# A hybrid diffusion step on one core: neighbourhood-attention values computed token-major

## The chip, the cores and the metric

The kernel runs on one core of one Trainium2 chip. The metric is the device time of one execution in microseconds (us). TensorE is called PE here, ScalarE ACT, VectorE DVE, GpSimd POOL, and SyncE, whose queue issues the transfers, SP.

## What is computed

Two trunk layers act on 384 tokens of 1024 features: 128 context tokens and 256 latent tokens. Each layer has a gated feed-forward, a mixer of three parallel branches, and a second feed-forward, each followed by a layer norm. The change concerns branch B of the mixer, attention over a 2-D neighbourhood with 8 heads of 64. Its queries, keys and values come from one input projection, and the values are also an output for the context tokens:

```python
z = h @ w_in
qb, kb, vb = jnp.split(zb, 3, axis=-1)          # zb: the 1536 columns of z for branch B
s = einsum(q, k) * SCALE + bias                 # latent: local window and cached context keys
p = softmax(s); o = einsum(p, v)                # context: full attention over the context
new_na_v = vb of the context tokens
```

## The kernel before

Activations lie feature-major: tile c holds features 128c to 128c+127 on the partitions and the 384 tokens along them. A projection of 128 output features is 8 chunks of 128 input features. Every product is made from two parts of each factor, high and low in the format float32r, as three matmuls: high by high, high by low, low by high. So a projected tile is 24 matmuls with a 128 x 128 weight block stationary and 384 tokens moving (`mm3_steps`, L391; `proj`, L1150). It is issued in four steps of two chunks, and each step reports a cost of 0.96 us to the plan.

Weights are one stream of 128 x 128 blocks in the order of their use (`Stream`, L341). A unit of eight blocks is fetched by one DMA (`raw`), copied by ACT into its high part (`hi`) and subtracted by DVE into its low part (`lo`). Two units of `hi` and `lo` are held, so ACT splits a new unit once PE has made the last product with an old one.

PSUM has eight banks, given out under three tags (L331 to L338): `mm`, three banks, for the dense products; `at`, three, for scores and outputs of the attention; `rw`, two, for transposes and others.

In the mixer, `attention` (L1089) takes eight pairs of heads, 0 to 3 of branch A and 4 to 7 of branch B. A pair (`heads_pair`, L1021) is a generator of eight parts: context scores, latent scores of head 0, transposes, context output, latent scores of head 1, transposes twice, and the output. Between the parts the plan puts steps of dense products. `XP` (L60) lists the dense tiles, first those ahead of the pairs and then those of iterations 0 to 8: "n" is the next projection that a coming pair needs (from `branch_a` and `branch_b`), "c" a projection of branch C with its convolution (`conv_gen`, L1254), "g" a gate, "p" a tile of branch A's output projection. Every letter counts as one tile of 3.84 us ("p" as a half); the sum is spread over eight steps by the weights `WY` (L61), and what is left at the end of an iteration is issued at once. A dense step is issued behind the attention's last instruction on PE so far. Pair m+1 is started in the last of the eight steps of iteration m; if its projections are not yet made, dense steps are issued until they are. The tile scheduler below this sets the final order on each engine.

For each pair of branch B, `branch_b` (L1205) makes three projections: keys (K), values (V) and queries (Q), numbered 0 to 3. The values come out feature-major in PSUM; ACT copies them to `vxb` (L1233), a DMA writes the context part out (L1234), and `token_major` (L990) transposes them with three 128 x 128 transposes on PE into a bank of `rw`, from which ACT copies `vt`, token by feature, which the pair's outputs read. K, V and Q of one pair are three letters "n". The convolution tiles come in the order of `C_FIRST` (L69): tw, al, k0, r0, v0, k1, r1, v1; the norms of a key tile (`kss`, a square root on ACT, L1286) are made within the tile that follows it.

Of the kernel before, what the change touches and what calls it, by code (L numbers as in the profile page):

```python
# [15 lines left out]
P = 128  # L16
# [43 lines left out]
XP = ('gggggg','nc','nggc','nc','nnnc','nnnpppppppp','nnn','nnnc','cc','c')  # L60
# [131 lines left out]
# sets of four groups of 256 modulations; the first two are what the first chunks of features need, then the others  # L192
# [3 lines left out]
def _layout(inp):  # L196
    """Rearranges the inputs (permutations and concatenations only)."""
# [36 lines left out]
    # [l][d][h = (p, e)][v][k] -> [l][(e, k)][p][d][v]  # L234
# [8 lines left out]
def _weights(inp, order):  # L243
    """The large weights as 128 x 128 blocks in the order of their use."""
    f = {k: np.asarray(inp[k]) for k in {o[0] for o in order}}
    arows = np.concatenate([_a_q_cols(m) for m in range(4)])
    n = len(order)
    assert n == WS_UNITS * UNIT
    ws = np.empty((WS_UNITS, P, UNIT, P), next(iter(f.values())).dtype)
    for i, (name, l, k, c) in enumerate(order):  # L250
        rows = arows[P * k : P * k + P] if name == "proj_a" else np.arange(P * k, P * k + P)
        cols = _a_q_cols(c[1]) if isinstance(c, tuple) else slice(c, c + P)
        ws[i // UNIT, :, i % UNIT] = f[name][l, rows][:, cols]
    return ws.reshape(WS_SHAPE)
# [7 lines left out]
    "o_vb": (DEPTH, 4, P, P),  # L262
# [4 lines left out]
def _unlayout(r):  # L267
# [7 lines left out]
    st = r["o_st"].reshape(DEPTH, 2, HD, 4, 2, HD)  # l, e, k, p, d, v  # L275
    st = np.ascontiguousarray(st.transpose(0, 4, 3, 1, 5, 2).reshape(DEPTH, 2, 8, HD, HD))[None]
    return (yp, ys, heads(r["o_ka"], 2), heads(r["o_va"], 2), heads(r["o_kb"], 8), heads(r["o_vb"], 8), st)


class Engine:  # L280
    """An engine that knows its last instruction."""
# [14 lines left out]
def trunk(tc, I, O, order, taps=None, stop=None):  # L296
# [5 lines left out]
    def then(*engines):  # L302
        """Behind the last instruction so far of these engines."""
# [37 lines left out]
    class Stream:  # L341
# [5 lines left out]
        def take(self, name, l, col, n, k0=0):  # L347
            order.extend((name, l, k, col) for k in range(k0, k0 + n))
            while len(self.left) < n:
# [5 lines left out]
            got, self.left = self.left[:n], self.left[n:]  # L355
            return got

        def ahead(self):
            """Out of the steady state: the unit after the next is split as soon as the last is used up."""
            if len(self.left) <= UNIT and self.unit < WS_UNITS:  # L360
                self.fetch(self.offset)
# [4 lines left out]
        def fetch(self, offset=0):  # L366
# [8 lines left out]
            for j in range(0, UNIT * P, n):  # L375
                V.tensor_tensor(out=lo[:, j : j + n], in0=raw[:, j : j + n], in1=hi[:, j : j + n].bitcast(F32), op=ALU.subtract)
            for i in range(UNIT):
                self.left.append((hi[:, i * P : (i + 1) * P], lo[:, i * P : (i + 1) * P]))
# [3 lines left out]
    def mm3(out, chunks, xs, after=()):  # L382
        """out += sum of W_k^T x_k, with both factors as sums of two float32r parts."""
# [7 lines left out]
    def mm3_steps(out, chunks, xs, step=2):  # L391
        """mm3 in steps of a few chunks, with what each costs."""
# [10 lines left out]
    def split(dst_h, dst_l, src, lo_eng):  # L403
        """src (SBUF or PSUM, float32) = dst_h + dst_l."""
# [30 lines left out]
    def ada_beside(pool, n):  # L435
        """The next n steps with the products on the vector engine: where that has time, and the tensor engine has not."""
# [38 lines left out]
    def ada_flush():  # L475
        """To columns: out[feature, (block, group, stream)]."""
# [20 lines left out]
    ax = [act.tile([P, NTOK], F32, name=f"ax{c}") for c in range(KD)]  # L497
    # (four more columns: see Norm)
# [8 lines left out]
    class Norm:  # L507
        """Layer norm over the features of y = alpha x + gate * out, chunk by chunk as out comes.
        The next phase's input is h = rs g1 (y - mu) + b1, g1 and b1 per feature and stream, rs and mu per token. Its
        first products W^T h run on z = g1 y, before rs and mu are known: rs W^T z - rs mu W^T g1 + W^T b1, with g1 and  # L510
        b1 as four more columns of z."""
# [34 lines left out]
        def add(self, c, po):  # L546
# [4 lines left out]
            if c == 0:  # L551
                # the table of Sqrt is there when it is needed
# [27 lines left out]
        def pilot(self):  # L580
            # about the mean of the first four chunks
# [14 lines left out]
        def products(self, chunks, xs, c):  # L596
            """The products of chunk c of out."""
# [14 lines left out]
        def finish(self, head=iter(())):  # L612
            """head: products of the next phase, in steps, from those on z to the last before h is needed."""
# [47 lines left out]
        def h(self, pool, c):  # L661
            """The next phase's input, in two parts."""
# [11 lines left out]
        def x(self):  # L674
            """alpha times the norm's output."""
# [5 lines left out]
    class Head:  # L681
        """The first products of a phase, on z: two groups of them, each chunk by chunk."""
# [25 lines left out]
        def begin(self, pool, norm, job, at):  # L708
            """The start of the phase: h follows the second group's products chunk by chunk; the first group's results."""
# [37 lines left out]
        def scaled(self, key, out, scale=1.0):  # L747
            """out = rs W^T z - rs mu W^T g1; returns scale W^T b1, a column per stream."""
# [21 lines left out]
    def gated(i, l, name, pool, xs, head, after):  # L770
        """128 features of silu(a) g, in two parts."""
# [70 lines left out]
    axd = es.enter_context(tc.tile_pool(name="axd", bufs=1, space=bass.MemoryType.DRAM))  # L842

    def mixer(l, nxt, next_head, head):
        spill = axd.tile([P, KD, NTOK], F32, name=f"axd{l}")
        gcd = axd.tile([P, KD, NTOK], F32, name=f"gcd{l}")
        with ExitStack() as st:
# [9 lines left out]
            with tc.tile_pool(name=f"rw{l}", bufs=1) as pool:  # L857
# [3 lines left out]
                def add(cost, until=None):  # L861
                    """Queues dense work behind the scans' last instruction."""
# [31 lines left out]
    def gate(l, i, m, th, head=None):  # L894
        """tanh(z / 2): the sigmoid is (1 + tanh(z / 2)) / 2."""
# [12 lines left out]
    def project(l, name, m, th, os):  # L908
        """2 merged += 2 gate * (o @ proj); the gate of branch A is in place."""
# [11 lines left out]
    def front_fill(l, keep, pool, w, oa, need, head):  # L921
        """The dense products beside the attention: what its next pair needs, then others."""
# [12 lines left out]

        for plan in XP:
            yield sum(todo[x][0] if x in todo else 1 for x in plan), some(plan)
# [6 lines left out]
    def mixer_fill(l, keep, pool, w, ob, gcd):  # L944
        """Projections without a place in a chain: they keep the tensor engine busy beside the scans."""
# [12 lines left out]
    def softmax(pool, views, nk, sinks):  # L958
        """views: score tiles [P, nk] in PSUM; sinks: [P, n or 1] or None."""
# [22 lines left out]
    def transposed(pe, nk, pts):  # L982
        """pts: P^T destinations [P, nk // P, P]."""
# [6 lines left out]
    def token_major(pool, src, tag):  # L990
        """[128 features, 384 tokens] -> [token, block, feature]."""
# [10 lines left out]
    def key_stack(pool, src, e, bufs):  # L1002
        """Keys of one head, src[64 e :, :384], as [hi; hi] and [lo; lo] over the 128 partitions."""
# [9 lines left out]
    def query_stack(pool, src, e):  # L1013
        """Latent queries of one head, src[64 e :, :256], as [hi; lo] (in either order)."""
# [6 lines left out]
    def heads_pair(pool, q_ctx, q_lat, k_ctx, kst, vt, v_cache, bias, sinks, keep, name, done, backward=False):  # L1021
        """Two heads (on partitions 0..63 and 64..127) of both streams -> o^T split in two parts."""
        # context queries: full attention over the context
# [9 lines left out]
        # latent queries: latent keys, then the cached context keys  # L1033
# [44 lines left out]
    def rope(pool, src, dst):  # L1078
        """Rotates the latent columns of src [128, 384] into dst [128, 256]."""
# [9 lines left out]
    def attention(l, pool, keep, w, oa, ob, head, spill):  # L1089
        """Branches A and B, pair of heads by pair of heads, among steps of the dense products."""  # L1090
# [37 lines left out]
        for m in range(9):  # L1128
# [3 lines left out]
            # two pairs at a time: the first part of one before the end of the other  # L1132
# [31 lines left out]
    def branch_a(l, pool, ready, soon, head):  # L1164
        """Windowed grouped-query attention; pair m has the query heads m and m + 4."""
# [38 lines left out]

    def branch_b(l, pool, ready, soon):  # L1205
        """Neighbourhood attention; latent queries in reverse order: the bias is then a forward walk through na_rpb."""
        cvb = pool.tile([P, 4, P], F32, name="cvb")
        nc.sync.dma_start(out=cvb, in_=I["cvb"][l].rearrange("p (a b) -> p a b", b=P))
        for m in range(4):
# [21 lines left out]
            pz = yield from proj(l, B_V0 + P * m, "pvb")  # L1231
            vx = pool.tile([P, NTOK], F32, tag="vx", bufs=1, name="vxb")
            S.activation(out=vx, in_=pz[:, :NTOK], func=AF.Copy)  # L1233
            nc.sync.dma_start(out=O["o_vb"][l, m], in_=vx[:, :NCTX])  # L1234
            vt = []
            soon.append([LATE, lambda vt=vt, vx=vx: vt.append(token_major(pool, vx, "vt"))])
            yield 0.96
            yield 0.0
# [8 lines left out]
            ready[4 + m] = (qx[:, :NCTX], qx[:, NCTX:], kc, kst, vt[0], cvb[:, m], bias, None)  # L1247
# [4 lines left out]
    C_INDEX = {n: i for i, n in enumerate(["tw", "al", "gl"] + [f"{x}{i}" for x in "krv" for i in range(4)])}  # L1252

    def conv_gen(l, keep, pool, w, names):  # L1254
        """Projections of the scans' inputs with the short convolution over time."""
        wsh = vcol(l, "w_shift")
        late = []
        for nm in names:
# [17 lines left out]
            elif nm[0] == "k":  # L1276
                # 1 / max(|k k_k|, 1e-12) per token and head
# [25 lines left out]
    def head_sums(out, sq):  # L1303
        """out[token, (block, head)] = sums of sq [128 features of two heads, 384] over each head."""
# [3 lines left out]
    def head_spread(pool, rn):  # L1308
        """[token, (block, head)] -> the same for each feature of the head, [128 features, 384], in PSUM."""
# [15 lines left out]
    def beside(k, m, n):  # L1325
        """Dense work beside a product: the tensor engine slows down where it has too little."""
# [464 lines left out]
```

## Time and profile before

| | |
|---|---|
| median of 3 runs | 2436.55 us (2436.5 to 2436.74) |
| span of the profiled execution | 2439.6 us |
| PE busy | 2297.4 us, 94% |
| DVE, ACT, POOL busy | 1696.6, 1056.4, 550.0 us |
| PE's share of the chain that ended last | 71% |

The page gives no time of the profiled execution besides its span. Matmuls are pipelined: a matmul's duration is longer than the distance between the starts of two, so work on PE is counted by starts. An idle time in brackets in the order of time is that of the engine before the instruction, with what ended it.

### The profile page before, as it was taken

How to read it: one execution, taken by the hardware profiler on the slowest of the kernel's cores; microseconds unless marked ns; L12 is line 12 of the kernel's file. 1: busy time of each engine (PE TensorE's matmuls, PEld its weight loads, DVE VectorE, ACT ScalarE, POOL GpSimd, SP SyncE). 2: the span in 40 equal slices, each digit the busy share in tenths (PEclk: the TensorE clock that was granted, in tenths of full speed). 3: DMA queues.
4: the chain of work that ended last, by engine and by line, in shares of the span. 5: the costliest groups of instructions: out<-in, count | busy, mean ns of one | idle time of the engine just before them, and what ended most of it. 6: DMA issues, size and time to landing. Idle time of an engine off the chain costs nothing.

```text
span 2439.6 us, 42863 instructions
## 1 busy us (share of the span) xinstructions
PE 2297.4 (94%) x17066; PEld 2106.5 (86%) x17066; DVE 1696.6 (70%) x2865; ACT 1056.4 (43%) x1942; POOL 550.0 (23%) x522
## 2 busy tenths in 40 slices
PE   7999999998899998999999999899989999999998
PEld 5999988897777788999889999889877777889997
DVE  3797886777767568786978954776787674665534
ACT  3333245655545445333243332555555454443332
POOL 2111422101122044211432113310022220542113
PEclk9999999999999999999999999999999999999999
DMA  8575644242111262665546743523321113534332
GB/s 314 193 240 198 191 122 130 84 111 78 40 57 47 72 209 95 191 217 180 180 147 205 244 130 122 154 81 91 112 70 39 51 50 90 204 102 140 130 121 87
DMA packets 125079, 324.54 MB, mean 133 GB/s; under 512 B 31568, under 2 KB 50256, under 8 KB 124880
## 3 DMA queue, kind: packets, MB, share of 16 engines
q1 hardware_dynamic: 124880, 321.81, 41.1%
q8 instruction: 134, 2.20, 0.4%
q14 instruction: 65, 0.53, 0.1%
HBM read 312.06 MB, written 9.70 MB: 132 GB/s over the span
## 4 chain that ended last, share of the span: by engine, by line
PE 71%; DVE 15%; ACT 5%; issue 4%; DMA 3%; POOL 2%; SPq 0%; POOLq 0%; ACTq 0%; DVEq 0%
PE po L399 5%; PE po L398 5%; PE po L397 5%; PE pa L387 4%; PE pg L389 4%; PE pa L388 4%; PE pg L387 4%; PE pg L388 4%; PE pa L389 4%; DVE lo L290 3%; DVE acc L290 2%; PE pz L397 2%; DMA adaw<-wada 2%; ACT hi L290 2%; PE pz L398 2%
## 5 line engine op out<-in xcount | busy, mean ns | idle before, releaser
L290 DVE TENSOR_TENSOR lo<-raw,hi 128x1024 fp32r<-128x1024 f32 (+1 forms) x472 | 583.8, 1246 | 305.9 <-ACT hi L290 303.8
L290 ACT ACTIVATE hi<-raw 128x1024 fp32r<-128x1024 f32 x418 | 441.7, 1058 | 785.0 <-issue 267.5
L290 DVE SCALAR_TENSOR_TENSOR acc<-adaw,cs,acc 128x1024 f32<-128x1024 f32 x224 | 292.3, 1327 | 0.0
L290 POOL TENSOR_TENSOR ul<-si,uh 128x384 fp32r<-128x384 f32 x88 | 126.3, 1435 | 579.3 <-ACT uh L290 579.3
L399 PE MATMUL po<-uh,lo 128*128 128x384 f32 x704 | 238.6, 339 | 6.3 <-DVE lo L290 6.3
L397 PE MATMUL po<-uh,hi 128*128 128x384 f32 x704 | 239.7, 340 | 0.0
L398 PE MATMUL po<-ul,hi 128*128 128x384 f32 x704 | 238.0, 338 | 0.0
L387 PE MATMUL pg<-zh,hi 128*128 128x384 f32 x656 | 224.1, 342 | 9.1 <-DVE si L290 9.1
L388 PE MATMUL pg<-zl,hi 128*128 128x384 f32 x656 | 223.8, 341 | 0.0
L389 PE MATMUL pg<-zh,lo 128*128 128x384 f32 x656 | 223.2, 340 | 0.0
L387 PE MATMUL pa<-zh,hi 128*128 128x384 f32 x632 | 216.2, 342 | 4.9 <-ACT si L290 4.4
L389 PE MATMUL pa<-zh,lo 128*128 128x384 f32 x632 | 213.8, 338 | 0.6 <-DVE lo L290 0.6
L388 PE MATMUL pa<-zl,hi 128*128 128x384 f32 x632 | 214.2, 339 | 0.0
L399 PEld LDWEIGHTS po<-uh,lo 128*128 128x128 f32 x704 | 133.5, 190 | 7.3 <-DVE lo L290 7.3
L397 PE MATMUL pz<-zh,hi 128*128 128x384 f32 x352 | 128.1, 364 | 8.5 <-ACT hi L290 5.7
L397 PEld LDWEIGHTS po<-uh,hi 128*128 128x128 f32 x704 | 133.7, 190 | 2.2 <-issue 0.8
L398 PEld LDWEIGHTS po<-ul,hi 128*128 128x128 f32 x704 | 133.5, 190 | 1.4 <-issue 0.8
L387 PEld LDWEIGHTS pg<-zh,hi 128*128 128x128 f32 x656 | 125.0, 191 | 10.0 <-ACT hi L290 6.7
L399 PE MATMUL pz<-zh,lo 128*128 128x384 f32 x352 | 126.3, 359 | 4.1 <-DVE lo L290 4.0
L387 PEld LDWEIGHTS pa<-zh,hi 128*128 128x128 f32 x632 | 119.1, 188 | 9.8 <-ACT si L290 5.3
L389 PEld LDWEIGHTS pg<-zh,lo 128*128 128x128 f32 x656 | 125.6, 191 | 1.6 <-issue 1.6
L388 PEld LDWEIGHTS pg<-zl,hi 128*128 128x128 f32 x656 | 125.0, 191 | 1.6 <-issue 1.6
(390 smaller groups left out, 5157.4 us busy)
## 6 DMA issues: line engine op xcount, KB each, us to landing
raw<-ws SPq DMA_DIRECT2D x418, 512.0 KB, 3.5
adaw<-wada SPq DMA_DIRECT2D x144, 512.0 KB, 4.8
bm<-rpb SPq DMA_DIRECT2D x64, 64.0 KB, 7.1
axd<-ax SPq DMA_DIRECT2D x16, 192.0 KB, 5.2
gcd<-gt SPq DMA_DIRECT2D x16, 192.0 KB, 4.7
gc<-gcd SPq DMA_DIRECT2D x16, 192.0 KB, 3.4
ax<-axd SPq DMA_DIRECT2D x16, 192.0 KB, 4.8
xt<-xt SPq DMA_DIRECT2D x8, 192.0 KB, 8.6
```

The costliest lines, as they stand in the source:

```text
L290: self.last = f(*a, **k)
L387: T.matmul(out, wh, xh, start=(k == 0), stop=False)
L388: T.matmul(out, wh, xl, start=False, stop=False)
L389: T.matmul(out, wl, xh, start=False, stop=(k == n - 1))
L397: T.matmul(out, wh, xh, start=(k == 0), stop=False)
L398: T.matmul(out, wh, xl, start=False, stop=False)
L399: T.matmul(out, wl, xh, start=False, stop=(k == n - 1))
```

## The change

The values of all four pairs of a layer are computed at once by a new function, `values_b`. The activations are stationary, 128 tokens of one chunk of features at a time, and the weights of 512 output features are moving. There are three banks, one for each block of 128 tokens, held through all eight chunks: 72 matmuls of 512 columns a layer instead of 96 of 384. The result is token-major, so ACT copies the three banks into `vb` and no transposes follow. One DMA of 256 KB a layer writes the output for the context tokens, instead of four of 64 KB. The weight stream takes the blocks in another order (`take_wide`: four neighbouring blocks of one chunk), as many as before. `values_b` runs in front of the queries of the first pair of branch B, in eight steps that report 1.92 us each, and counts as one letter "n". The plan `XP` is changed with it. All other lines of the diff take out comments. The core of it:

```diff
-XP = ('gggggg','nc','nggc','nc','nnnc','nnnpppppppp','nnn','nnnc','cc','c')
+XP = ('gggggg','nc','nggc','nc','nnn','nnpppppppp','nnc','nnc','cc','c')
...
-    "o_vb": (DEPTH, 4, P, P),
+    "o_vb": (DEPTH, P, 4 * P),
...
+        def take_wide(self, name, l, k, col):
+
+            order.extend((name, l, k, col + P * i) for i in range(4))
+            self.need(4)
+            (hi, lo), i = self.left[0][2]
+            assert i % 4 == 0
+            del self.left[:4]
+            return hi[:, i * P : (i + 4) * P], lo[:, i * P : (i + 4) * P]
...
+    def values_b(l, vb):
+
+        pvs = [mmp("pvb") for _ in range(3)]
+        for k, (zh, zl) in enumerate(hs):
+            wh, wl = stream.take_wide("w_in", l, k, B_V0)
+            for t, pv in enumerate(pvs):
+                q = slice(P * t, P * t + P)
+                T.matmul(pv, zh[:, q], wh, start=(k == 0), stop=False)
+                T.matmul(pv, zl[:, q], wh, start=False, stop=False)
+                T.matmul(pv, zh[:, q], wl, start=False, stop=(k == KD - 1))
+            if k < KD - 1:
+                yield 1.92
+        for t, pv in enumerate(pvs):
+            S.activation(out=vb[:, t], in_=pv, func=AF.Copy)
+        nc.sync.dma_start(out=O["o_vb"][l], in_=vb[:, 0])
+        yield 1.92
...
+        vb = pool.tile([P, 3, 4 * P], F32, name="vb")
...
-            pz = yield from proj(l, B_V0 + P * m, "pvb")
-            vx = pool.tile([P, NTOK], F32, tag="vx", bufs=1, name="vxb")
-            S.activation(out=vx, in_=pz[:, :NTOK], func=AF.Copy)
-            nc.sync.dma_start(out=O["o_vb"][l, m], in_=vx[:, :NCTX])
-            vt = []
-            soon.append([LATE, lambda vt=vt, vx=vx: vt.append(token_major(pool, vx, "vt"))])
-            yield 0.96
-            yield 0.0
+            if m == 0:
+                yield from values_b(l, vb)
+                yield 0.0
...
-            ready[4 + m] = (qx[:, :NCTX], qx[:, NCTX:], kc, kst, vt[0], cvb[:, m], bias, None)
+            ready[4 + m] = (qx[:, :NCTX], qx[:, NCTX:], kc, kst, vb[:, :, P * m : P * m + P], cvb[:, m], bias, None)
```

`Stream.take` keeps its meaning; the fetching of units is now in `Stream.need`, and each block remembers its unit and its place in it, for `take_wide`.

## Rows read from the trace of the kernel before

**Rows 1.** Page, its first line and busy time by engine.

```profile
span 2439.6 us, 42863 instructions
...
PE 2297.4 (94%) x17066; PEld 2106.5 (86%) x17066; DVE 1696.6 (70%) x2865; ACT 1056.4 (43%) x1942; POOL 550.0 (23%) x522
```

**Rows 2.** Stretches of both attention stages; the first line names the columns.

```profile
core 0: us, PE busy (x) PEld busy (x) DVE busy (x) ACT busy (x) POOL busy (x), PEclk, DMA share, GB/s
...
442.20:447.20 5.00, 4.91 (x18) 3.85 (x18) 3.17 (x13) 2.95 (x9) 0.00 (x0) 0.66 0.01 2
...
468.00:503.00 35.00, 35.00 (x208) 32.76 (x207) 21.60 (x49) 20.04 (x43) 0.00 (x0) 1.00 0.36 104
...
503.00:526.00 23.00, 23.00 (x144) 20.80 (x143) 15.60 (x34) 13.57 (x33) 2.38 (x1) 1.00 0.45 119
...
526.00:549.00 23.00, 21.62 (x129) 19.23 (x127) 16.99 (x35) 14.37 (x40) 2.55 (x1) 1.00 0.45 118
...
1730.00:1753.00 23.00, 21.10 (x126) 19.16 (x127) 16.71 (x35) 13.80 (x38) 2.60 (x1) 1.00 0.36 113
```

**Rows 3.** Value tile: duration min/median/max (ns), first and last start, form.

```profile
L397 PE MATMUL pvb<-zh,hi x64: 332/337/450, 454.0 to 1742.4; 128*128 128x384 f32 x64
...
L290 ACT ACTIVATE vxb<-pvb x8: 472/472/488, 461.0 to 1744.7; 128x384 f32<-128x384 f32 x8
```

**Rows 4.** Order of time (start, us, engine, line, what): PE around one transpose.

```profile
460.05 0.33 PE L397 MATMUL pqb<-zh,hi 128*128 128x384 f32 x1
...
462.13 0.49 PE L994 MATMUL vt<-con,vxb 128*128 128x128 f32 x3
...
462.38 0.42 PE L397 MATMUL pqb<-zh,hi 128*128 128x384 f32 x1
...
462.64 0.34 PE L398 MATMUL pqb<-zl,hi 128*128 128x384 f32 x1
...
464.54 0.82 PE L987 MATMUL pt<-con,pe 128*128 128x128 f32 x6
...
465.12 0.42 PE L397 MATMUL pc<-zh,hi 128*128 128x384 f32 x1
```

**Rows 5.** Order of time: pair 4's last key product, ACT after it.

```profile
453.66 0.34 PE L399 MATMUL pkb<-zh,lo 128*128 128x384 f32 x1
...
454.07 1.06 ACT L290 ACTIVATE hi<-raw 128x1024 fp32r<-128x1024 f32 x1
...
455.54 0.41 ACT L290 ACTIVATE krb<-pkb 128x256 f32<-128x256 f32 x1
```

**Rows 6.** Order of time: pair 6's last query product and what follows.

```profile
524.85 0.34 PE L399 MATMUL pqb<-zh,lo 128*128 128x384 f32 x1
...
526.01 0.53 ACT L290 ACTIVATE qxb<-pqb 128x128 f32<-128x128 f32 x2
...
526.35 0.49 PE L1027 MATMUL sc<-kc,qxb 64*128 64x128 f32 x4
...
528.22 0.86 PE L1067 MATMUL po<-ptl,vt 128*64 128x256 f32 x5 [1.38 <-ACT ptl L290]
```

**Rows 7.** Order of time on ACT: table loads around k0's norms.

```profile
467.58 1.28 ACT L290 ACT_TABLE_LOAD   x1
...
469.07 1.28 ACT L290 ACT_TABLE_LOAD   x1
```

**Rows 8.** Order of time on PE: end of the stage, pair 7.

```profile
570.38 0.65 PE L1067 MATMUL po<-ptl,vt 128*64 128x256 f32 x2 [1.82 <-ACT ptl L290]
```

**Rows 9.** Order of time on PE where pair 3 starts.

```profile
442.17 0.48 PE L1027 MATMUL sc<-kx,qx 64*128 64x128 f32 x2 [2.83 <-ACT pe L290]
...
443.75 0.69 PE L397 MATMUL pc<-zh,hi 128*128 128x384 f32 x1
...
445.84 1.27 PE L987 MATMUL pt<-con,pe 128*128 128x128 f32 x6
...
447.22 0.44 PE L1039 MATMUL sl<-kh,qs 128*128 128x384 f32 x1
```

More of the change, by code (lines that the diff above doesn't have):

```diff
@@ L276, in _unlayout @@
     st = np.ascontiguousarray(st.transpose(0, 4, 3, 1, 5, 2).reshape(DEPTH, 2, 8, HD, HD))[None]
-    return (yp, ys, heads(r["o_ka"], 2), heads(r["o_va"], 2), heads(r["o_kb"], 8), heads(r["o_vb"], 8), st)
+    vb = np.ascontiguousarray(r["o_vb"].reshape(DEPTH, P, 8, HD))[None]
+    return (yp, ys, heads(r["o_ka"], 2), heads(r["o_va"], 2), heads(r["o_kb"], 8), vb, st)
 class Engine:
@@ L348, in take, with need @@
             order.extend((name, l, k, col) for k in range(k0, k0 + n))
+            self.need(n)
+            got, self.left = self.left[:n], self.left[n:]
+            return [g[:2] for g in got]
+        def need(self, n):
             while len(self.left) < n:
@@ L354, in take @@
                     self.fetch(self.offset)
-            got, self.left = self.left[:n], self.left[n:]
-            return got
+        def take_wide(self, name, l, k, col):
[5 more added lines that the diff above has]
+            return hi[:, i * P : (i + 4) * P], lo[:, i * P : (i + 4) * P]
         def ahead(self):
@@ L376, in fetch @@
                 V.tensor_tensor(out=lo[:, j : j + n], in0=raw[:, j : j + n], in1=hi[:, j : j + n].bitcast(F32), op=ALU.subtract)
+            whole = (hi, lo)
             for i in range(UNIT):
-                self.left.append((hi[:, i * P : (i + 1) * P], lo[:, i * P : (i + 1) * P]))
+                self.left.append((hi[:, i * P : (i + 1) * P], lo[:, i * P : (i + 1) * P], (whole, i)))
     stream = Stream()
@@ L936, in front_fill @@
         for plan in XP:
-            yield sum(todo[x][0] if x in todo else 1 for x in plan), some(plan)
+            tiles = sum(todo[x][0] if x in todo else 1 for x in plan)
+            yield (tiles + 3 if plan == "nnn" else tiles), some(plan)
     def gate_c(l, keep, m, gcd):
```

## The prediction

> **What bounds the kernel now.** I read the head of the page, then the table of stretches, then the order of time on TensorE. The page has PE at 94% of a span of 2439.6 us [rows 1]. Branch B's values are computed inside the attention of each layer, where pairs of heads and dense products alternate. There are two such stages; the second does the same work some 1204 us later, so I work with the first. From 468 us on, PE's busy time equals the stretch, 35.00 of 35.00 and 23.00 of 23.00 us, at clock 1.00; only the stretch from 526 to 549 us has a hole, 21.62 of 23.00, and in the second stage its counterpart, 21.10 of 23.00 [rows 2]. So here PE's issue order sets the end: a us that PE need not issue is a us gained, unless a wait takes its place. DVE and ACT are busy three quarters of these stretches or less, and their work matters only where PE waits for it.
>
> Busy times overlap, so I count by starts. Twelve matmuls of 384 columns start from 460.05 to 462.13: 0.173 us each, though each lasts 0.34 [rows 3, 4]. That slot is my unit.
>
> **Transposes that go.** Before, each of 8 blocks (4 a layer) is brought to token-major by three transposes. They start at 462.13 and the next product at 462.38, which is 0.25 us; that product then holds its slot for 0.26 instead of 0.173 [rows 4]. So 0.34 us a block, 2.7 us for 8, all on the path: **-2.7**. With them go 16 copies on ACT (0.47 us each for the block [rows 3], about the same for its transpose) and 6 of the 8 output DMAs; three copies of 512 columns and one DMA come per layer. Nobody waits for those, so I cost them at nothing; ACT's cover is the dense products beside it, and if that cover is gone, ACT's saving (some 2 us a layer) would still be on the good side.
>
> **Products that change shape.** Per layer, 96 matmuls of 384 columns (16.64 us by the slot) become 72 of 512. The columns are the same, 36,864. No matmul of 512 columns in this number format is in the trace, so bounds: if the slot grows with the columns, 0.231 us and nothing is gained; if it lies on the line from the 128-column transposes (six in 0.58 us, 0.097 each [rows 4]) through 0.173 at 384, it is 0.211 and 15.2 us, a gain of 1.4 a layer. I take a value near the upper end, because its row is of the same kind of product and the transposes are another kind: at the full level of 2.4 GHz one column a pulse (my assumption) would be 160 of the 173 ns, and if the other 13 are fixed per instruction, 512 columns take 0.227 us, 72 of them 16.3: **-0.6** for both layers, bounds -2.9 and 0.
>
> The Trainium skill (TensorE: Matmul & The Clock Gate, Back-to-back issue gap) gives N / 2.4 + 2.5 ns. At 384 columns that is 162.5 ns, and the trace has 173, so the rule is short by 11 ns here. By it 512 columns would take 216 ns and the term would be -2.2 (an estimate from that page) instead of -0.6.
>
> **Weights.** A unit of eight blocks feeds 24 matmuls of 384 before, 18 of 512 after: 4.16 and about 4.1 us. Fetch, split and DMA keep their pace, and both plans take the same number of units: nothing.
>
> **A wait that comes: three banks at once.** The dense products rotate over three PSUM banks, one tile at a time, so a tile has a whole tile's time to be emptied. The values hold all three. The first matmul of the third token block needs the bank of the key tile K0 just before. That comes 0.173 + 6 x 0.227 = 1.53 us after K0's last matmul has started. Before, that matmul starts at 453.66; ACT first splits a weight unit (1.06 us, from 454.07), and K0's second copy ends at 455.54 + 0.41 = 455.95, which is 2.29 later [rows 5]. So PE waits 0.76 us, and its whole queue, dense and attention, waits behind that matmul. Two layers: **+1.5**. Bounds: nothing, if the attention's own matmuls are placed in the hole; 1.8 a layer, if another split of 1.06 goes ahead of the copies.
>
> At the other end Q0 needs one bank. The first token block is finished six matmuls (1.36 us) before the last, and its copy takes some 0.57 us (the copies of 256 and 384 columns take 0.41 and 0.47 [rows 3, 5], carried on): hidden, 0. If a split goes ahead of it, up to 1.1 a layer.
>
> **The pacing.** The plan counts a tile as 3.84 us of dense work to spread over eight steps of the pairs. Before, iterations 3 to 6 carry 4, 7, 3 and 4 tiles. After, they carry the work of 6, 6, 3 and 3, but the value tile is counted as one though it costs 15.36. So iteration 3 spreads three tiles over its steps and issues the rest, half the values and Q0, in one run before pair 4 starts. Three tiles a step-round are enough: the stretch 503 to 526 has this pace and PE is busy throughout [rows 2]. What matters is what stands behind the query tile when a pair starts. Before, iteration 5 ("nnn") has nothing there: Q2's last matmul starts at 524.85, ACT copies it from 526.01, the scores of pair 6 follow at 526.35, and then PE sits idle for 1.38 us, since the output of pair 5 waits for copies that stand behind the query tile's on ACT [rows 6]. After, iteration 5 ends with a convolution tile and this hole is covered, but iteration 3 loses its convolution tile and pair 4 starts as pair 6 did. -1.4 and +1.4 a layer: **0**, bounds -1.4 and +1.4 a layer, as one or the other hole proves covered by late attention work.
>
> **A table load that moves.** The convolution tile r0 carries the norms of k0, whose square root makes ACT load two tables, 1.28 us each [rows 7]. Before, that falls into iterations 3 and 4 with dense work behind it and costs PE nothing; the same pair of loads at the end of the stage leaves PE idle for 1.82 us before pair 7's products [rows 8]. After, it falls into iterations 5 and 6, where one dense step instead of two lies between the parts of a pair. Bounds 0 and 1.8 a layer. I take **0**: again a convolution tile and then a key tile stand behind it, as in iteration 3, and not the end of the stage.
>
> **Sum.** -2.7 - 0.6 + 1.5 = -1.8 us. The trace is of an execution whose span is 2439.6; the page gives no other time for it, and it lies 3.05 above the median of 2436.55. The terms are differences, so I take them from the median: 2434.7.
>
> **Rivals.** (1) *Short slots and no bank wait.* The 512-column slot is the line's 0.211 and attention matmuls fill K0's wait: -2.7 - 2.9 = -5.6, 2430.9. For it: PE's order is made by a scheduler that moves ready work forward. Against it: a transpose is not this kind of product. 0.15.
>
> (2) *Banks and tables.* K0's wait 1.8 and Q0's 1.1 a layer, and half the table price in each layer: -2.7 - 0.6 + 3.6 + 2.2 + 1.8 = +4.3 at the worst; about half way between that and the forecast is its middle, 2438. For it: in the rows, the split stands ahead of the copies [rows 5]. Against it: ACT has slack. The Trainium skill (Perfetto Trace Analysis, Identifying Performance Opportunities) reads a gap that repeats on the saturated engine as too few buffers, PSUM among them; before, no such gap repeats at the value tiles, so no row here bears that out yet. 0.17.
>
> (3) *The clock falls at pair 4: slower.* Where pair 3 starts, PE has been idle for 2.83 us by the row, and then six dense matmuls take 2.09 us (443.75 to 445.84) instead of 1.04 [rows 9]; in the stretch from 442 us the granted clock is 0.66 [rows 2], a part of it at the lower level of 1.2 GHz. The transposes behind them take 1.38 instead of 0.58 [rows 4, 9]. If pair 4's start, with nothing dense behind it, idles as long, it costs 2.83 + 1.05 + 0.8 = 4.7 a layer: 9.4 - 1.8 = +7.6, 2444.1. It decides from an idle near 2.8 us; at pair 6's 1.38 us the clock stayed at 1.00 [rows 2]. Pair 4 starts like pair 6, and pair 3's case also had branch A's rotation in the chain, so 0.08.
>
> That the transposes stay is excluded: no call of them is left for branch B.
>
> **How the numbers follow.** Forecast 0.60, rivals 0.15, 0.17, 0.08. A measurement of this kernel tells about 0.2%, 4.9 us, from no change: 2431.7 and 2441.4. Forecast and rival (2) lie within, (1) is faster, (3) slower: 0.15, 0.77, 0.08. The range reaches from just below (1)'s value, 2430.5, to 2440.0, above most of (2). It leaves out (3) and the rims of (1) and (2), together below 0.2.
>
> **What would show it.** Twelve transposes a layer gone and 72 matmuls of 512 columns at starts 0.227 us apart: if 0.21 or 0.23, that term moves to its bound. One hole of about 0.8 us among the first six value matmuls after K0. PE idle of about 1.4 us at pair 4 and none at pair 6, clock 1.00 at both. The table loads for k0 beside pairs 5 and 6 without a hole on PE. The prediction is wrong if the clock drops in the stretch of pair 4, if PE waits between the values and Q0, or if stages outside the attention change length, since I expect them to be moved in time alone.

## The result, and the profile after

| | before | after |
|---|---|---|
| median, timed in turn on one chip | 2438.52 us (2436.5 to 2445.99, 6 runs) | 2459.39 us (2453.44 to 2467.96, 6 runs) |
| ratio, with 95% interval | | 1.0083 (1.0065 to 1.0101) |
| span of the profiled execution | 2439.6 us | 2466.2 us |

The change makes the kernel 0.8% slower. I had forecast 2434.7 us and a range up to 2440.0; the time is far above it, on the side that I gave 0.08.

The head of the page after answers to [rows 1]:

```profile
span 2466.2 us, 42705 instructions
...
PE 2314.5 (94%) x16994; PEld 2113.1 (86%) x16994; DVE 1693.3 (69%) x2865; ACT 1054.1 (43%) x1932; POOL 554.0 (22%) x522
```

PE has 72 matmuls less (24 transposes and 48 products) and yet 17 us more of busy time. That points to a slower clock for some of its work; the granted clock of the stretches below shows it.

To place the 26.6 us I cut both spans at instructions that both kernels have: the first matmul of K0 (`pkb`), the first `up` of the stage behind the attention, and the first mixer product behind that. The table of stretches of the kernel before (two attention stages, then the two stages behind them; columns as in [rows 2]):

```profile
448.02:577.56 129.54, 125.35 (x751) 112.35 (x750) 86.49 (x210) 78.38 (x186) 5.53 (x5) 1.00 0.36 102
1651.43:1781.84 130.41, 125.69 (x751) 112.63 (x750) 86.41 (x206) 77.88 (x184) 5.57 (x5) 1.00 0.35 102
577.56:886.59 309.03, 285.36 (x3540) 237.70 (x3540) 217.09 (x443) 152.63 (x282) 69.92 (x95) 0.98 0.22 71
1781.84:2088.43 306.59, 283.69 (x3541) 235.94 (x3541) 217.59 (x443) 152.67 (x282) 70.45 (x95) 0.98 0.23 71
```

The same stretches of the kernel after:

```profile
445.77:583.59 137.82, 128.85 (x715) 110.79 (x714) 89.12 (x215) 77.47 (x181) 5.68 (x5) 0.97 0.34 100
1660.17:1799.27 139.10, 129.55 (x714) 111.35 (x713) 89.55 (x211) 76.98 (x179) 6.67 (x5) 0.96 0.33 99
583.59:891.57 307.98, 286.56 (x3541) 239.36 (x3541) 213.34 (x437) 152.41 (x281) 72.77 (x95) 0.97 0.21 69
1799.27:2116.79 317.52, 294.75 (x3540) 245.98 (x3540) 214.15 (x437) 152.66 (x281) 71.12 (x95) 0.94 0.20 67
```

The attention stages are 8.3 and 8.7 us longer, together 17.0 of the 26.6. They lose PE twice: it is idle more (9.0 of 137.8 us against 4.2 of 129.5), and the granted clock is 0.97 and 0.96, where it was 1.00. Counted from the records of the clock, PE spent 8.9 and 10.2 us of them at the lower of its two levels (1.2 of 2.4 GHz), against 0 and 0.2 before. The stage behind the second attention is 10.9 us longer at clock 0.94, though its instructions on PE are the same in the same order. I take the attention first.

Each of these rows is one execution. How far one kernel's executions lie apart is shown by experiment 7 further down, which turned out to be the kernel before in effect:

```profile
447.64:580.11 132.47, 128.34 (x750) 114.32 (x749) 86.22 (x206) 77.82 (x184) 5.67 (x5) 0.97 0.34 100
1653.77:1785.69 131.92, 127.21 (x750) 113.29 (x749) 86.51 (x210) 78.49 (x186) 5.51 (x5) 0.99 0.34 100
```

So an attention stage of the kernel before varies by up to 3 us along with the clock (7.0 and 3.4 us at the lower level here), and the 137.8 and 139.1 us after lie clearly above that. The profiled execution after is also the slowest of its six (2467.96 us against a median of 2459.39), so a part of the 26.6 us is its own.

**The value block is not where it goes.** PE in the order of time (start, us, engine, line, what) around the values of layer 0:

```profile
452.77 0.39 PE L1229 MATMUL pvb<-lo,zh 128*128 128x512 f32 x1
453.00 0.38 PE L1002 MATMUL pt<-con,pe 128*128 128x128 f32 x2
453.13 0.48 PE L1227 MATMUL pvb<-hi,zh 128*128 128x512 f32 x1
...
453.92 0.39 PE L1227 MATMUL pvb<-hi,zh 128*128 128x512 f32 x1
...
457.87 0.40 PE L1229 MATMUL pvb<-lo,zh 128*128 128x512 f32 x1
...
470.23 0.39 PE L1229 MATMUL pvb<-lo,zh 128*128 128x512 f32 x1
470.46 0.34 PE L411 MATMUL pqb<-zh,hi 128*128 128x384 f32 x1
...
475.98 0.49 PE L1042 MATMUL sc<-kc,qxb 64*128 64x128 f32 x4
477.84 0.86 PE L1082 MATMUL po<-ptl,vt 128*64 128x256 f32 x5 [1.38 <-ACT ptl L291]
```

From 453.92 to 457.87 there are 17 slots of 512 columns, 0.232 us each. The third block's first matmul, which had to wait for K0's bank, follows two transposes at 453.13 without a gap, and Q0 follows the last value matmul after 0.23 us. The hole at pair 4 is there as forecast, 1.38 us idle at 477.84, and the clock stays up.

**It goes at the later pairs.** Where pair 6 starts, before there was one idle of 1.38 us [rows 6]. After:

```profile
526.63 0.34 PE L413 MATMUL pc<-zh,lo 128*128 128x384 f32 x1
526.80 0.82 PE L1002 MATMUL pt<-con,pe 128*128 128x128 f32 x6
527.55 0.49 PE L1042 MATMUL sc<-kc,qxb 64*128 64x128 f32 x2
529.01 0.49 PE L1042 MATMUL sc<-kc,qxb 64*128 64x128 f32 x2 [0.98 <-ACT pe L291]
530.24 1.06 PE L1082 MATMUL po<-ptl,vb 128*64 128x256 f32 x2 [0.74 <-ACT ptl L291]
531.24 1.54 PE L1002 MATMUL pt<-con,pe 128*128 128x128 f32 x6
533.36 1.54 PE L1082 MATMUL po<-ptl,vb 128*64 128x256 f32 x5 [0.58 <-ACT ptl L291]
...
535.26 0.69 PE L1054 MATMUL sl<-kh,qs 128*128 128x384 f32 x1
...
536.71 0.52 PE L411 MATMUL pkb<-zh,hi 128*128 128x384 f32 x1
```

From 526.80 to 536.71 there is no dense product at all. PE waits for ACT at each part of the pairs, the clock falls at 530.3 us for 6.83 us, and from there the six transposes last 1.54 us instead of 0.82. In this stretch the kernel before had a query tile, here already issued. The same waits come at pair 7 (PE idle 0.74 and 0.75 us; the clock stays up) and at the end of the stage, where PE is idle for 2.27 us at 581.17 and the clock falls at 581.5 for 3.41 us. They come again in the second layer, where the clock falls at pairs 6 and 7.

**Why the dense work is gone by then.** Two things in the plan do this.

The first is a line that I overlooked. The section on the change says that the value block counts as one letter "n" and that all other lines of the diff take out comments. That is untrue: besides the unpacking of the output, `front_fill` also has

```diff
-            yield sum(todo[x][0] if x in todo else 1 for x in plan), some(plan)
+            tiles = sum(todo[x][0] if x in todo else 1 for x in plan)
+            yield (tiles + 3 if plan == "nnn" else tiles), some(plan)
```

so iteration 3 is counted as six tiles and spreads 23.04 us of work over its eight steps.

The second is in `attention`, in lines that the diff doesn't touch. The plan adds each step's share to `debt` and takes off what each dense step costs. But `start(m + 1)` also issues dense steps, until the pair's projections are made, and takes nothing off. In iteration 3 after, the last three steps of Q0 (2.88 us) are issued in this way. The last of the eight steps then adds its share of 3.07 us, of which 0.19 was issued ahead, and finds nothing left to issue: 2.88 us stay as debt. This debt is never repaid and goes on to iterations 4 to 8: each begins 2.88 us in debt, issues its first dense tile at once in its first step, and runs out before the next pair starts. The kernel before has the same flaw, but carries only 0.96 us, from iteration 5 on. Worked through step by step, the rule gives the order that both traces show.

### The profile page after: what moved, and what is told of

Its sections match the earlier page's. It is cut to its first block, busy times and chain, and to the rows that moved or that the text cites. A ratio compares the mean times of both kernels' runs of the same rounds, so it can differ in the third digit from the quotient of the medians.

```text
span 2466.2 us, 42705 instructions
## 1 busy us (share of the span) xinstructions
PE 2314.5 (94%) x16994; PEld 2113.1 (86%) x16994; DVE 1693.3 (69%) x2865; ACT 1054.1 (43%) x1932; POOL 554.0 (22%) x522
## 4 chain that ended last, share of the span: by engine, by line
PE 70%; DVE 15%; ACT 6%; issue 4%; DMA 3%; POOL 2%; SPq 0%; POOLq 0%; DVEq 0%; ACTq 0%
PE po L413 5%; PE po L412 5%; PE po L411 5%; PE pg L401 4%; PE pa L401 4%; PE pg L403 4%; PE pg L402 4%; PE pa L402 4%; PE pa L403 4%; DVE lo L291 3%; DVE acc L291 2%; ACT hi L291 2%; DMA adaw<-wada 2%; PE pz L411 2%; PE pz L412 2%
## 5 line engine op out<-in xcount | busy, mean ns | idle before, releaser
L291 DVE TENSOR_TENSOR lo<-raw,hi 128x1024 fp32r<-128x1024 f32 (+1 forms) x472 | 581.5, 1242 | 309.8 <-ACT hi L291 308.6
L291 POOL TENSOR_TENSOR ul<-si,uh 128x384 fp32r<-128x384 f32 x88 | 126.2, 1434 | 580.8 <-ACT uh L291 580.8
```

The source lines that it names most:

```text
L291: self.last = f(*a, **k)
```

## Experiments

Theory A: the unpaid steps of iteration 3 are the cause. Theory B: the wide products are, by their slots, their banks or their unit copies.

**1. After, with the debt forgotten at the end of each iteration.**

```diff
             while step(fill) is not None:
                 pass
+            debt = min(debt, 0.0)
```

> The kernel after, with one line more: at the end of each iteration of the attention a debt of dense work that is left over is forgotten. After the change the three query steps that are issued to start pair 4 are not taken off the debt, so 2.88 us are owed from iteration 3 on and each later iteration issues its dense tiles early and has none left at its end. Theory A (the debt): the stretch from the first key product of branch B to the first decay product goes from 138 us back to 128 to 131 in each layer, and the kernel takes 2432 to 2442 us, within 0.3% of before. Theory B (the wide products or the three banks held cost the time): the stretch stays at 135 or more and the kernel at 2453 to 2468 us.

Measured: 2445.49 us, ratio to before 1.0024 (1.0006 to 1.0043). Its stretches, in the same order:

```profile
448.00:577.44 129.44, 123.93 (x714) 107.69 (x713) 86.46 (x210) 75.62 (x180) 5.38 (x5) 1.00 0.36 102
1653.81:1782.95 129.14, 123.92 (x714) 107.70 (x713) 85.77 (x210) 75.48 (x180) 5.73 (x5) 1.00 0.35 103
577.44:886.60 309.16, 286.59 (x3541) 238.87 (x3540) 216.00 (x443) 153.91 (x283) 71.00 (x95) 0.97 0.22 70
1782.95:2094.98 312.03, 288.69 (x3541) 240.57 (x3541) 215.94 (x443) 153.92 (x283) 70.99 (x95) 0.96 0.22 70
```

One line gives back 8.4 and 10.0 us of the attention stages, with clock 1.00 in both. The stages are where theory A put them; the kernel's time is 3.5 us above the 2442 us that it gave as the upper end. At pair 6 dense products (`pc`) now stand behind the scores, and PE's longest idle there is 0.67 us:

```profile
528.11 0.49 PE L1042 MATMUL sc<-kc,qxb 64*128 64x128 f32 x4
528.53 0.44 PE L411 MATMUL pc<-zh,hi 128*128 128x384 f32 x1
...
532.75 0.44 PE L1054 MATMUL sl<-kh,qs 128*128 128x384 f32 x1 [0.67 <-ACT pe L291]
```

**2. Before, with one tile of debt added in iteration 3.** If theory A is right, the kernel before must become slow without any wide product.

```diff
+            debt += 3.84 if m == 3 else 0.0
```

> The kernel before, values feature-major and transposed, with 3.84 us added to the debt at the end of iteration 3 of the attention and nothing else. Theory A (the debt): iterations 4 to 8 issue their dense tiles one tile earlier, PE has holes at the end of iterations 5 and 6, and the kernel is slower by 8 to 20 us (2445 to 2460). Theory B: it stays within 3 us of before.

Measured: 2454.83 us, ratio 1.0056 (1.0037 to 1.0075). The attention stages:

```profile
448.07:584.99 136.92, 129.34 (x750) 114.85 (x750) 89.16 (x215) 79.02 (x186) 6.36 (x5) 0.98 0.34 101
1655.63:1792.56 136.93, 129.29 (x750) 114.98 (x749) 87.27 (x215) 78.93 (x186) 6.17 (x5) 0.98 0.34 101
```

They are 7.4 and 6.5 us longer than before, with 6.8 us at the lower level in each. PE is idle for 1.61 us where pair 6 starts (528.07 us) and twice for 0.75 us at pair 7, as expected at the end of iterations 5 and 6. The loss of the attention stages can be put in and taken out without touching the products. For it theory A stands and B falls. The stage behind the second attention is not much longer here (308.0 us), so its 10.9 us in the kernel after are not shown to come from the debt.

**3. The values behind the first query, not in front of it.** To experiment 1 this adds a move of `values_b`, so that Q0 is made before pair 4 is to start and no step is issued unpaid; worked through step by step, no debt is left here, and the line of experiment 1 has nothing to do.

```diff
-            if m == 0:
-                yield from values_b(l, vb)
-                yield 0.0
...
             ready[4 + m] = (...)
+            if m == 0:
+                yield from values_b(l, vb)
+                yield 0.0
```

> As the kernel after with the debt forgotten, and the values computed behind the queries of branch B's first pair instead of in front of them, so that dense work lies behind pair 4's start. Theory A: the hole of about 1.4 us where pair 4 starts goes in each layer, 2 to 4 us under the version with the debt forgotten alone. Theory B: no difference of more than 1 us to that version.

Measured: 2441.27 us, ratio 1.0005 (0.999 to 1.002). The attention stages:

```profile
450.76:577.93 127.17, 123.67 (x715) 107.68 (x714) 85.62 (x210) 75.62 (x180) 5.42 (x5) 1.00 0.37 104
1647.14:1776.90 129.76, 125.25 (x714) 108.99 (x713) 87.29 (x210) 75.70 (x180) 5.36 (x5) 0.99 0.36 102
```

PE no longer idles at pair 4, in either layer. The stages are 2.4 and 0.7 us shorter than before, which is within the spread between executions, and against experiment 1 only the first is shorter. The kernel is 4.2 us faster than in experiment 1, a little more than theory A gave, but it isn't faster than before.

**4. Before, with the debt forgotten** (the line of experiment 1), to see what this line does by itself.

> The kernel before with a debt left over forgotten at the end of each iteration; there it is 0.96 us from iteration 5 on. Theory A: a small debt, so within 3 us of before either way. Theory B says nothing of it: no difference.

Measured: 2441.41 us, ratio 1.0004 (0.9988 to 1.002), with attention stages of 132.3 and 131.6 us, like those of experiment 7. The line is no gain by itself, so experiment 1 took away the fault of the change and not something that all kernels pay.

**What is left: a table load?** In experiments 1 and 3 the last square root of the attention comes behind the last exponential, so ACT has to load a table on the way from `up` to the tanh that follows it. ACT in the order of time in experiment 1:

```profile
577.55 1.28 ACT L291 ACT_TABLE_LOAD   x1
578.85 0.58 ACT L291 ACTIVATE th<-up,hb 128x384 f32<-128x384 f32 x1
```

Some 17 us later PE waits for a product of DVE and POOL, `bk`. In the kernel before, then in experiment 1:

```profile
594.29 0.87 PE L1340 MATMUL pb<-con,bk 128*128 128x128 f32 x6 [1.31 <-POOL bk L290]
```

```profile
595.18 0.87 PE L1369 MATMUL pb<-con,bk 128*128 128x128 f32 x6 [2.19 <-POOL bk L291]
```

By starts PE loses 1.64 and 2.52 us there. Theory C: the load causes this longer wait, and the wait a fall of the clock. Theory D: it does not; the rest lies in the wide products or is chance.

I tried to move the load with a one-column activation behind the last two parts of pair 7, and to bring it into the kernel before with a square root:

```diff
                     next(pairs[m - o])
+                    if m == 8:
+                        S.activation(out=pool.tile([P, 1], F32, tag="warm", bufs=1, name="warm"), in_=C("leps"), func=AF.Tanh)
```

> Kernel: the one of e1_after_paid, plus a one-column Tanh on ACT behind each of the last two parts of pair 7, so that the activation table that `up` needs is loaded while ACT is idle ahead of the last o3h. Theory C (what e1 still loses is a table load): in e1 the last Sqrt (rn, 569.85) came behind the last Exp (568.34), so ACT loaded a table for 1.28 us at 577.55, on the way from `up` to th; VectorE then ran 0.9 us late, PE waited 2.52 us for bk at `pb` (before: 1.63), and the clock fell 3 us later, in both layers. With the load moved the wait at `pb` is 1.6 us again, no clock drop comes some 19 us behind `up`, the stretch from `up` to the mixer's output has 10 to 17 us at the low clock (e1: 17.1 and 23.9), and the ratio to the kernel before is 0.998 to 1.001. Theory D (the rest is in the wide products, or is chance): the wait and the drops stay, ratio 1.002 to 1.004 as e1.

> Kernel: the one of e3_values_last with the same early Tanh. Theory C: the stretch from K0 to `up` as in e3 (127.2 and 129.8 us; 129.5 and 130.4 before), `pb` waits 1.6 instead of 2.53 us, the drops 19.7 us behind `up` go: 2 to 5 us below e3, ratio 0.997 to 1.000, the version that has the transposes' 2 us a layer. Theory D: as e3, 1.0005, within 0.999 to 1.002.

> Kernel: the kernel before plus a one-column Sqrt on ACT behind each of the last two parts of pair 7, so that the first Tanh behind `up` must load its table again, as in e1. Theory C: a table load of 1.28 us near 577.6 and 1781.9, `pb` waits 2.5 instead of 1.63 us, clock drops some 19 us behind `up` in both layers, 3 to 7 us slower: ratio 1.001 to 1.003. Theory D: the load is hidden (VectorE is not what `pb` waits for) and the ratio is 0.999 to 1.001.

Measured: ratios 1.0006 (0.9991 to 1.002), 1.0003 (0.9987 to 1.0019) and 1.0009 (0.9994 to 1.0023). None of them tests theory C. The operation read a constant, the scheduler moved it to 345.9 us, and the table load stayed where it was (575.55 us in the first of the three). So they repeat experiments 1 and 3 and the kernel before, and as such they are of use: the 1.0024 of experiment 1 became 1.0006.

The second attempt reads the last output, `o3h`, and so can't be moved ahead of it:

```diff
                     next(pairs[m - o])
+                    if m == 8 and len(ob) == 4:
+                        S.activation(out=pool.tile([P, 1], F32, name="warm"), in_=ob[3][0][:, NTOK - 1 :].bitcast(F32), func=AF.Tanh, scale=0.0)
```

> Kernel: the one of e1_after_paid, plus a one-column Tanh on ACT that reads the last o3h, so that it can't be moved ahead of the last Sqrt (in e5_paid_table it read a constant and ran at 345.9 us instead; the table load stayed at 575.55, so that e5 was a second look at e1). The load then falls into ACT's idle time behind o3h (1.64 us in e1, from 574.4) . Theory C (the load at `up`, 1.28 us, is what e1 and e3 still pay): th runs 0.3 us behind the first `up` as in the kernel before, PE's wait at `pb` is 1.0 to 1.7 us instead of 2.52, the drops of the clock 18 to 20 us behind `up` (seen behind five of the eight 2.5 us waits of e1, e3, e5 and e6, and behind none of 1.65) are gone, ratio 0.998 to 1.001. Theory D (it is not): ratio 1.0006 to 1.0024 as e5 and e1.

(That text miscounts: four of the six waits of 2.5 us in these four kernels were followed by a fall 18 to 20 us behind `up`, not five of eight. And th starts 0.94 us behind `up` in the kernel before, not 0.3.)

> Kernel: the one of e3_values_last with the same Tanh behind the last o3h. Theory C: K0 to `up` 127 to 129 us (before 129.5 and 130.4), `pb` waits at most 1.7 us, no drop 18 to 20 us behind `up`; ratio 0.997 to 0.9995. Theory D: 1.0003 to 1.0005 as e6 and e3, since the length of the later stages varies by more than the 1 to 2 us a layer that are saved.

> Kernel: the kernel before plus a one-column Sqrt on ACT that reads the last o3h (in e7_before_late_table it read a constant, ran early, and the load did not come), so that the first Tanh behind `up` loads its table again. Theory C: two more table loads a layer, one of them near `up`, `pb` waits 2.5 us instead of 1.63, drops 18 to 20 us behind `up` in one or both layers, ratio 1.001 to 1.003. Theory D: the load moves the end by less than can be told, ratio 0.999 to 1.001.

Measured: the load is moved, to 573.64 us in the first of the three, and th starts 0.95 us behind `up`, as before. But the ratios are 1.0016 (1.0002 to 1.003) and 1.0011 (0.9994 to 1.0028): nothing is gained. The wait at `pb` becomes 2.03 to 2.07 us, not 1.6, and in the first of the three `spread` waits for 1.6 us ahead of `up` (by starts).

This is no clean test, for the added operation does more than move the load. Its one-column tile lies in the attention's memory, and the first operations of the next stage, `vv` and `gt`, are now released by it (`warm`): `vv` starts at 575.26 us, 126.9 behind K0's first matmul. In experiment 1 the last `po` released it, at 573.04, 125.0 behind K0. Other traces speak against theory C without it: in the kernel after and in experiment 2 no load stands behind `up`, and PE still loses 2.07 to 2.41 us at `pb`. So the load is not the only cause of the longer wait. What it costs by itself is not shown, and theory D isn't told apart.

The third, the kernel before with two table loads more a layer, came out at 2457.37 us, ratio 1.0069 (1.0044 to 1.0094). The engines in the order of time:

```profile
576.32 1.28 ACT L290 ACT_TABLE_LOAD   x1
...
577.61 0.20 ACT L290 ACTIVATE warm<-o3h 128x1 f32<-128x1 f32 x1
...
577.94 1.36 POOL L290 COPY vv<-v 128x384 f32<-128x384 f32 x1 [37.38 <-ACT warm L290]
578.04 0.70 DVE L290 MEMSET gt<- 128x768 f32 x1 [1.28 <-ACT warm L290]
...
579.66 1.28 ACT L290 ACT_TABLE_LOAD   x1
...
581.31 0.30 PE L1342 MATMUL spread<-con,rb 128*128 128x128 f32 x1 [3.78 <-DMA gu<-gup]
```

Its attention stages are 4.4 us longer each (133.92 and 134.78), PE stands idle for 3.8 us ahead of `spread`, and the stages behind have clock 0.95 and 0.96. But `pb` waits for 1.41 us there, less than before. The next stage begins late: `vv` starts at 577.94 behind `warm`, 128.7 us behind K0, in the kernel before at 574.19 behind `po`, 126.2 behind K0. What `spread` reads, `rb`, comes at 580.66, since DVE splits a weight unit first (`lo`, 1.59 us from 578.87). So the loss is that of an operation in the attention's memory that itself waits for a load; neither theory had described it, and it is no price of a load alone.

**Time against the clock.** The 79 runs of the kernel before that stood beside experiments 1 to 10 differ in the granted clock of the whole run, and their time falls by 1.63 us for each 0.001 of it. That is 4.9 us more or less at the lower level, so each us at that level goes with about 0.33 us of time (an estimate: the line joins clock and time and does not say which moves which). Mean difference of each kernel's runs from that line (0 is the kernel before at the same clock; after was timed beside other runs of it than these 79):

| | at equal clock | mean clock |
|---|---|---|
| after | +10.7 us | 0.976 |
| experiment 2, before with debt | +8.1 | 0.978 |
| experiment 1, after with debt forgotten, and its repeats 5 and 8 (8 with the load moved) | +0.9, -2.8, +1.4 | 0.978, 0.979, 0.980 |
| experiment 3, values last, and its repeats 6 and 9 (9 with the load moved) | -2.9, -6.2, -2.3 | 0.979, 0.978, 0.979 |
| experiment 4, before with debt forgotten; 7, the kernel before in effect | +1.2, +0.4 | 0.981, 0.982 |
| experiment 10, before with two more loads | +7.7 | 0.976 |
| kernel before | 0 | 0.982 |

By this line the version with the values last would at the same clock be faster than the kernel before by 2 to 6 us, about the gain that the change was to bring. Experiments 3 and 6, the same kernel in effect, differ by 3.3 us here, so that is a hint and no measurement. What gives it back is a clock that is lower by 0.003, some 5 us by the same line. Where that clock is lost I have found in part only. One place is the wait at `pb`: over the profiles of all twelve kernels, the clock fell 17 to 20 us behind `up` after 8 of the 14 waits of 2.0 to 2.6 us there (by starts), and after none of the 10 waits of 0.9 to 1.7. That is a coincidence in the traces, and no run has changed this wait alone; why DVE comes later there in most of these kernels stays open. Nor does one length of wait decide. Where the last part of pair 7 begins, the kernel before waits for 1.82 us in both layers (570.38 [rows 8] and 1774.66) and the clock stays up; in experiment 7 it waits as long, and the clock falls in both, first at 570.7 us:

```profile
570.11 0.65 PE L1067 MATMUL po<-ptl,vt 128*64 128x256 f32 x2 [1.82 <-ACT ptl L290]
570.68 1.54 PE L987 MATMUL pt<-con,pe 128*128 128x128 f32 x6
```

No version that I ran beats the kernel before.

## Why the prediction was wrong

**Transposes, -2.7:** the term held in kind. They are gone and nobody waits for the copies. Its size is not shown: experiment 3's attention stages are 3.0 us shorter in sum than before, but the stages of one kernel vary by as much.

**The slot, -0.6:** mis-sized, at its upper bound. Measured are 0.232 us for 512 columns, beside 0.175 for 384 in Q0 behind it (23 slots from 470.46 to 474.48): the slot grows with the columns, and the term is 0. My split of the 173 ns into 160 for the columns and 13 fixed had no row behind it. The rule of the Trainium skill (TensorE: Matmul & The Clock Gate, Back-to-back issue gap), N / 2.4 + 2.5 ns, which the page gives for an isolated matmul, gives 216 ns and was further off.

**K0's bank, +1.5:** wrong, it is 0 here. I took it that the values follow K0's last matmul at once. After, ten outputs of pair 2 stand between them, K0's copies end at 452.60 (the third line below), and two transposes fill the place where I saw a hole:

```profile
449.78 0.34 PE L413 MATMUL pkb<-zh,lo 128*128 128x384 f32 x1
450.05 0.86 PE L1082 MATMUL po<-ptl,vt 128*64 128x256 f32 x5
452.21 0.39 ACT L291 ACTIVATE krb<-pkb 128x256 f32<-128x256 f32 x1
```

My rival (1) had this case, by a scheduler that moves ready work forward. That holds for the two transposes, which the plan issues behind the first chunk of the values. The ten outputs stand there by the plan itself: with six tiles counted, K0's last steps are issued ahead of pair 2's last part, and the values behind it. **Q0's bank, 0:** right. (The copy of 512 columns took 0.59 us; the two rows that I carried on give 0.53, not 0.57.)

**The starts and the pacing, 0:** this step failed, and it decides the result. I counted the value tile as one, so that iteration 3 spreads three tiles, issues the rest before pair 4 and owes nothing. The code counts it as four: iteration 3 spreads six tiles, `start` issues Q0's last three steps unpaid, and 2.88 us of debt make iterations 4 to 8 run out of dense work. The runs showed attention stages 8.3 and 8.7 us longer, back at 129.4 and 129.1 us with the debt forgotten (experiment 1), and 7.4 and 6.5 us longer when a debt is put into the kernel before (experiment 2). The misread count decides here. Worked through with three tiles, the same rule leaves no debt, for `K0` and half the values, which are paid, cost 11.52 us, just three tiles; no run had this count. Half of the term came true: pair 4 starts with the idle of 1.4 us that pair 6 had. But I priced only which tile stands behind the query when a pair starts. The evidence was in the code of `front_fill` and `attention`: with the right count I should have carried one number, the debt, through all nine iterations. The bounds of 1.4 us a layer came from the one hole of the kernel before, and no row of it showed a stage that runs out of dense work.

**The table load of k0, 0:** right within its bounds; with the debt forgotten (experiment 1) the loads stand at 527.42 and 529.65 us, beside the start of pair 6, and the idle of PE behind them is the 0.67 us shown there.

**Rival (3), the clock falls:** right in sign and kind, wrong in place and rule. I placed it at pair 4, where the clock stayed up, and let it decide from one idle of 2.8 us. At pair 6 it fell after idles of 0.98 and 0.74 us with only some attention matmuls between them, at the end of the stage after 2.27 us. Its 4.7 us a layer was about half of the 8.3 and 8.7 measured. That its total of 2444.1 us lies on the right side is no credit to its reason.

**Stages outside the attention, moved in time alone:** wrong. The stage behind the second attention took 317.5 us instead of 306.6, with 37.5 us at the lower level instead of 10.2. Their order doesn't change, but their clock does. How much of it is the change and how much this execution is open: in experiment 6, too, one of the two stages has 315.4 us and the other 310.0.

## What to carry to other kernels

Where dense work is spread by a plan with an account, follow the account through the whole stage before you price a change of order: a step that is issued outside of it makes later iterations issue early and run dry where the cover is needed. Look for that stretch by its mark, attention matmuls on PE with no dense product between them and short waits at each. A saving of 2 us on PE is worth measuring only together with the clock, since 0.001 of granted clock over the run goes with 1.6 us here. And an operation that is added as a probe may hold memory that the next stage waits for: see in the trace who is released by it before its time is read as an answer.

## What was not expected of the hardware

- A matmul of 512 columns in float32r, with a weight load for each, starts every 0.232 us and one of 384 every 0.173 to 0.175: within 1% the ratio of the columns, so this kernel pays nothing per instruction that a wider product could save.
- The clock fell without a long idle: at 530.3 us after waits of 0.98 and 0.74 us, and in 8 of 14 cases behind a single wait of 2.0 to 2.6 us. Behind the same wait of 1.82 us at pair 7 it stayed up in both layers of one execution of the kernel before and fell in both layers of another (experiment 7).
- A one-column operation at the end of the attention, with two table loads of 1.28 us around it, made an attention stage 4.4 us longer, by way of the next stage's operations that it released late (`vv` 128.7 us behind K0 instead of 126.2).
